# Another order for the seven block products of a matrix stage, and no low parts made by an accumulating DMA

## The chip, the cores and the metric

The kernel runs on one core of a Trainium2 chip. Times are device microseconds (us) of one execution; the profile is one further execution, taken by the hardware profiler. Five engines matter: TensorE (PE in the profile, with its weight loads as PEld), VectorE (DVE), ScalarE (ACT), GpSimd (POOL) and SyncE (SP), which here only issues DMAs. Each engine runs its instructions in program order, one behind the other, and engines wait for each other through semaphores.

## The reference

One decoder layer on 256 tokens with a width of 1024, in float32: an RMS norm and an input projection; beside each other eight attention heads (causal, with norms and rotary tables on q and k) and a gated convolution branch; an output projection added to the input; then a second RMS norm and a gated feed-forward part with 2816 inner columns. The change lies in this last part alone:

```python
x = x + jnp.concatenate([attn, conv], axis=-1) @ w_out[l]
h = rms_norm(x, norm2_g[l])
x = x + (jax.nn.silu(h @ w_gate[l]) * (h @ w_up[l])) @ w_down[l]
```

## The kernel before

**Three matmuls for one.** A float32 product is computed from two parts of each operand: a high part, rounded to the format that TensorE takes, and a low part, which is the operand less its high part. `product` (L704) issues three matmuls for it: high by high, high by low, low by high. The weights arrive in float32, 1 MB a block of 128 x 2048, and are split on the chip in *pieces* of 1024 columns, two to a block ("a" and "b"). `feed` (L248) does that. For each piece ScalarE copies the high part (`wh`, L255), and later VectorE subtracts it from the raw block for the low part (`wl`, L264). A ring holds 7 pieces. When TensorE's program reaches piece p, `feed(p + 4)` is called: it issues high parts up to p + 5 and low parts up to p + 4, the high parts first.

**How a feed-forward chunk is done.** The 2816 inner columns are cut into six chunks: 0, 1, 2, 4 and 5 of 512 columns, 3 of 256. A plain chunk (`plain_units`, L871) needs, for each of gate and up, both halves of the 1024 inputs and both halves of the 256 tokens: 8 half-block units of one piece and 4 products each. Chunks 1 and 4 are done otherwise (`shared_units`, L890), with seven block products for eight, as in Strassen's and Winograd's scheme. The activations' two token halves and two input halves are four blocks; sums of them (`xsum(0)` to `xsum(3)`) are made once by VectorE and ScalarE in `xsums_task` (L817). The weights' four blocks are gate and up by input half; in the list of pieces (`_plan`, L75) they are called b11 and b21 (gate, first and second half of the inputs) and b12 and b22 (up). Their sums are made in place: b11 becomes b11+b12, then with b22 added, then with b21 added; b12 becomes b12+b22. A sum is made either by VectorE, just before the high part of the piece (`raw`, L254), or by an accumulating DMA from HBM, issued by GpSimd just behind the low part of the piece (`raw`, L267): in the tuples of `todo` the second entry is what VectorE adds, and a pair as the third entry tells what a DMA adds, and to which block, once the piece is split.

**The order of work in a shared stage.** The loop over `STAGES` (L918) alternates: one of the seven products (2 pieces, 2 products of three matmuls each a piece), then one unit of the plain chunk beside it (1 piece, 4 products), and a last plain unit. Chunks 1 and 2 make the first shared stage, chunks 4 and 5 the second. Numbered through the kernel from 0, the first shared stage is pieces 36 to 57, the second 62 to 83; chunk 0 is 28 to 35 and chunk 3 is 58 to 61, and the last matrix follows from 84. The seven products go into three PSUM banks: U (four products), V (two) and W (one). U and V are added to on and on, and between the products a copy or a difference is taken from the bank, before the next product may write to it: `s1` and `s2` are copies of U, `s5` is a copy of V, all by ScalarE; `c11` (line L841) is W + s1, `c12` (L850) is V - s2, `c22` (L857) is s5 - U, by VectorE. `c11` goes through a silu on ScalarE and with `c12` through `times` (L795, tile `ac`); `turned` (L783) transposes such a tile on TensorE (tile `aT`, four transposes), and ScalarE and VectorE split it again (`act`, L789 and L791).

**What is put where in the queues.** Small pieces of work of this kind are generators; `step()` runs what is due after every second product, so each engine's queue is a fixed list: `feed`'s splits with this work between them. At the start of the first shared stage there still come the results of chunk 0: `up2_task` puts its two `ac` behind the splits that `feed(41)` and `feed(42)` issue, and its transposes behind piece 38 and behind piece 39 in TensorE's queue. At the second shared stage those of chunk 3 stand in the like place: `ac` behind the splits of `feed(68)`, transposes within pieces 65 and 66.

**Low parts by DMA.** In a shared stage, two of the plain chunk's low parts are not made by VectorE (the mark `"low"` in `_plan`: pieces 41 and 53, then 67 and 79). ScalarE copies the high part with its sign turned (`wl`, L261), and GpSimd issues a DMA that adds the raw block to it (L262).

**Loads.** `loads` is the order in which SP issues blocks; `load_next` is called when a piece marked "load" or "low" has been split, and issues up to the next block that lives in the ring of four `raw` buffers. b11 and b12 have buffers of their own, and so has b22 ("side", one that it shares with the tile `full`, which `xsums_task` reads). SP's queue is in order too: an issue whose buffer is still read holds up those behind it.

Of the kernel before, what the change touches and what calls it, by code (L numbers as in the profile page):

```python
# [8 lines left out]
F32 = mybir.dt.float32  # L9
# [3 lines left out]
AF = mybir.ActivationFunctionType  # L13
# [3 lines left out]
P = 128  # L17
# [4 lines left out]
W = 512  # L22
# [45 lines left out]
def _halves(c):  # L68

    if c:  # L70
        return [(z, kh, half) for z in range(2) for kh in range(2) for half in range(2)]
    return [(z, kh, half) for kh in range(2) for z in range(2) for half in range(2)]


def _plan():  # L75

    base = 14
    block = {}
    for c, width in enumerate(WIDTHS):
        for z in range(2 if width == W else 1):  # L80
            for kh in range(2):
                block[c, z, kh] = base
                base += 1
    loads = [(i, "raw") for i in range(2, 14)]
    plain = lambda i: [(i, a, None, "load") for a in range(2)]
    sources = [p for i in range(14) for p in plain(i)]
    for stage in STAGES:
        second = [(block[stage[-1], z, kh], half) for z, kh, half in _halves(stage[-1])
                  if (stage[-1], z, kh) in block]
        second_pieces = [(i, half, None, "low" if len(stage) == 2 and j % 4 == 1 else "load")  # L90
                         for j, (i, half) in enumerate(second)]
        second_loads = [(i, "raw") for i, half in second if half == 0]
        if len(stage) == 1:
            loads += second_loads
            sources += second_pieces
            continue
        b11, b21, b12, b22 = (block[stage[0], z, kh] for z in range(2) for kh in range(2))
        loads += [(b11, "big_h"), (b12, "big_l"), (b21, "raw"), second_loads[0], (b22, "side")] + second_loads[1:]
        both = [(0, 1) for _ in range(7)]
        todo = [(b11, None, None), (b21, None, "load"), (b11, b12, (b12, b22)), (b22, None, None),  # L100
                (b11, b22, (b11, b21)), (b12, None, None), (b11, None, None)]
        for j in range(8):
            if j < 7:
                i, add, then = todo[j]
                sources += [(i, a, add, then) for a in range(2)]
            sources.append(second_pieces[j])
    for i in range(base, NB):
        loads.append((i, "raw"))
        sources += plain(i)
    return loads, sources  # L110
# [66 lines left out]
def _build(nc, tc, t, ctx):  # L177
# [3 lines left out]
    raw = pool("raw", RAW)  # L181
# [5 lines left out]
    def mm_bank(name, cols=512):  # L187
        return psum.tile([P, cols], F32, name=name, tag="mm", bufs=4)

    def t_bank(name, tag="t"):  # L190
        return psum.tile([P, 512], F32, name=name, tag=tag, bufs=2)
# [15 lines left out]
    def spawn(gen, wait=0):  # L207
        tasks.append([now[0] + wait, gen])
# [10 lines left out]

    blocks, pieces = {}, []  # L220
    loads, sources = _plan()

    def load_next():
# [47 lines left out]
    def wpart(j, a):  # L271
        return [p[:, a * W:(a + 1) * W] for p in pieces[j]]
# [107 lines left out]
    c = early.tile([P, NT + 2 * NT * H], F32, name="c")  # L380
# [56 lines left out]
    def root(part):  # L437
        seed(c[:, part], v[:, part])
        newton(c[:, part], v[:, part], ca[:, part])
# [240 lines left out]
    for h in range(H):  # L680
# [6 lines left out]
        o = O[pair // 2][base:base + HD, pair % 2, :]  # L687
# [12 lines left out]
    ffn = {"r": None}  # L700
# [3 lines left out]
    def product(bank, lhs, w, start, stop, on=False):  # L704

        for a, (l, r) in enumerate(((lhs[0], w[0]), (lhs[0], w[1]), (lhs[1], w[0]))):
            nc.tensor.matmul(bank, l, r, start=start and a == 0, stop=stop and a == 2, skip_group_check=on)  # L707
        ticks[0] += 1
        if ticks[0] % 2 == 0:
            step()  # L710
# [4 lines left out]
    def residual_task(i, n):  # L715
        cols = slice(n * W, n * W + W)
        nc.vector.tensor_tensor(x2[:, i, cols], po[i, n], x2[:, i, cols], op=ALU.add)
        sq = ffn["late"].tile([P, W], F32, name=f"sq{i}{n}", tag="sum", bufs=4)
        nc.scalar.activation(sq, x2[:, i, cols], AF.Square, accum_out=sums2[:, i, n:n + 1])
        yield 0  # L720

# [30 lines left out]
    late = ffn["late"] = late_pool[0] = pool("late")  # L752
# [25 lines left out]
    def silu(name, src, i, width=W):  # L778
        s = late.tile([P, W], F32, name=name, tag="sf", bufs=3)
        nc.scalar.activation(s[:, :width], src, AF.Silu, scale=ffn["r"][:, i:i + 1])  # L780
        return s

    def turned(c, i, u, nf):  # L783
        b = t_bank(f"aT{c}{i}").rearrange("p (a q) -> p a q", a=4)
        for a in range(nf):
            nc.tensor.transpose(b[:, a, :], u[:, a * P:(a + 1) * P], ident)  # L786
        f0 = STARTS[c] // P
        hi, lo = (acts[:, z, f0:f0 + nf, tok(i)] for z in range(2))
        nc.scalar.activation(hi, b[:, 0:nf, :], AF.Copy)  # L789
        yield 1  # L790
        nc.vector.tensor_tensor(lo, b[:, 0:nf, :], hi.bitcast(F32), op=ALU.subtract)  # L791

    def times(c, i, src, s, width=W):
        u = late.tile([P, W], F32, name=f"ac{c}{i}", tag="ac", bufs=2)
        nc.vector.scalar_tensor_tensor(u[:, :width], src, ffn["r"][:, i:i + 1], s[:, :width],  # L795
                                       op0=ALU.mult, op1=ALU.mult)
        return u
# [11 lines left out]
            yield from turned(c, i, ups[i], width // P)  # L809

    def part(name):
        return late.tile([P, W], F32, name=name, tag="sum", bufs=4)

    xs = [acts[:, z, NF - 8:, :].rearrange("p f (b q) -> p (f b) q", b=2).rearrange("p (s k) q -> p s k q", s=4)
          for z in range(2)]
# [16 lines left out]
    S = {}  # L832

    def copied(name, bank):
        S[name] = part(name)
        nc.scalar.activation(S[name], bank, AF.Copy)
        yield 0

    def gate_first(c, bank):
        g = part(f"c11{c}")  # L840
        nc.vector.tensor_tensor(g, bank, S["s1"], op=ALU.add)  # L841
        yield 1
        S["g0"] = silu(f"sg0{c}", g, 0)

    def up_first(c, U, V):
        S["s2"] = part(f"s2{c}")
        nc.scalar.activation(S["s2"], U, AF.Copy)
        yield 1
        u = part(f"c12{c}")
        nc.vector.tensor_tensor(u, V, S["s2"], op=ALU.subtract)  # L850
        u = times(c, 0, u, S["g0"])
        yield 2
        yield from turned(c, 0, u, 4)

    def up_second(c, bank):
        S["u1"] = part(f"c22{c}")
        nc.vector.tensor_tensor(S["u1"], S["s5"], bank, op=ALU.subtract)  # L857
        yield 0

    def gate_second(c, bank):  # L860
        g = silu(f"sg1{c}", bank, 1)
        yield 1
        u = times(c, 1, S["u1"], g)
        yield 2
        yield from turned(c, 1, u, 4)
# [3 lines left out]
    xsum = lambda j: [[z[:, j, k, :] for z in xs] for k in range(4)]  # L869
# [20 lines left out]
    def shared_units(c):  # L890

        U, V = (t_bank(f"{n}{c}", "s") for n in "UV")
        banks = {"U": U, "V": V}

        def unit(lhs, name, start, stop, after):
            if name == "W":
                banks["W"] = mm_bank(f"W{c}")
            for k in range(4):
                if k % 2 == 0:
                    feed(at[0] + LEAD)  # L900
                product(banks[name], lhs[k], wpart(at[0], k % 2), start and k == 0, stop and k == 3, not start)
                at[0] += k % 2
            if after:
                spawn(after(), EVICT)

        todo = ((block(0, 0), "U", True, True, lambda: copied("s1", U)),
                (block(1, 0), "W", True, True, lambda: gate_first(c, banks["W"])),
                (xsum(0), "V", True, True, lambda: copied("s5", V)),
                (xsum(3), "V", False, True, None),
                (xsum(1), "U", False, True, lambda: up_first(c, U, V)),  # L910
                (xsum(2), "U", False, True, lambda: up_second(c, U)),
                (block(1, 1), "U", False, True, lambda: gate_second(c, U)))
        return [lambda u=u: unit(*u) for u in todo]

# [3 lines left out]
    for stage in STAGES:  # L918
# [9 lines left out]
        else:  # L928
            c = stage[0]
# [14 lines left out]
    for f, i, n in order:  # L944
        if i == n == 0:
            feed(at + f + LEAD)
        product(pd[i, n], [acts[:, z, f, tok(i)] for z in range(2)], wpart(at + f, n), f == 0, f == NF - 1)
        if f == NF - 1:
            o = late.tile([P, W], F32, name=f"o{i}{n}", tag="sum", bufs=4)
            nc.vector.tensor_tensor(o, pd[i, n], x2[:, i, n * W:n * W + W], op=ALU.add)  # L950
            nc.sync.dma_start(t["out"][i][:, n * W:n * W + W], o)

# [58 lines left out]
```

## Time and profile before

| | |
|---|---|
| median of 3 runs | 298.17 us (297.9 to 298.96) |
| profiled execution, its own time | 298.19 us |
| its span | 296.4 us |
| around the span | 1.79 us |
| granted TensorE clock | 1.00 |
| TensorE busy with matmuls | 287.7 us of the span |
| VectorE busy | 208.0 us |
| ScalarE busy | 176.9 us |

The views used below: the page of the profile (busy time), a table of busy time by stretch of the span, the list of waits (who waited for whom, total, number of times, longest), the chain of work that ended last, and the timeline, whose rows give start, duration, engine, line, operation, output and inputs, and in brackets how long the engine had been idle and what ended that. A "xN" at the end of a timeline row is N instructions one behind the other, merged. A row of a VectorE instruction overlaps the next by under 0.1 us, so the spacing of starts is what one costs in the queue, not its duration.

### The profile page before, as it was taken

How to read it: one execution, taken by the hardware profiler on the slowest of the kernel's cores; microseconds unless marked ns; L12 is line 12 of the kernel's file. 1: busy time of each engine (PE TensorE's matmuls, PEld its weight loads, DVE VectorE, ACT ScalarE, POOL GpSimd, SP SyncE). 2: the span in 40 equal slices, each digit the busy share in tenths (PEclk: the TensorE clock that was granted, in tenths of full speed). 3: DMA queues.
4: the chain of work that ended last, by engine and by line, in shares of the span. 5: the costliest groups of instructions: out<-in, count | busy, mean ns of one | idle time of the engine just before them, and what ended most of it. 6: DMA issues, size and time to landing. Idle time of an engine off the chain costs nothing.

```text
span 296.4 us, 3672 instructions
## 1 busy us (share of the span) xinstructions
PE 287.7 (97%) x1333; PEld 231.7 (78%) x1333; DVE 208.0 (70%) x322; ACT 176.9 (60%) x266; POOL 25.1 (8%) x46
## 2 busy tenths in 40 slices
PE   8999999999999999999998999999989999999994
PEld 6888877778788888887786788887868888888883
DVE  3899995999972967999946838989288474444111
ACT  4776768989735677768549635667676263344000
POOL 0005372000000000003111000302100000000000
PEclk9999999999999999999999999999999999999999
DMA  7999868544603449399996991599677368400012
GB/s 251 418 413 355 313 250 313 199 142 150 277 10 133 144 163 404 109 399 190 294 206 145 426 425 81 168 181 310 126 216 313 112 205 324 174 2 0 0 63 78
DMA packets 12051, 62.83 MB, mean 212 GB/s; under 512 B 1601, under 2 KB 2209, under 8 KB 6274
## 3 DMA queue, kind: packets, MB, share of 16 engines
q1 hardware_dynamic: 9874, 54.86, 48.6%
q0 software_dynamic: 2016, 7.74, 13.6%
q8 instruction: 10, 0.16, 0.2%
q14 instruction: 7, 0.06, 0.1%
q10 hardware_dynamic: 144, 0.00, 0.0%
HBM read 59.46 MB, written 1.05 MB: 204 GB/s over the span
## 4 chain that ended last, share of the span: by engine, by line
PE 79%; DMA 8%; DVE 6%; ACT 4%; issue 2%; ACTq 0%
PE pd L707 20%; PE p L668 18%; PE fg L707 17%; DMA raw<-w 8%; PE po L707 7%; PE U L707 6%; DVE wl L264 2%; ACT wh L255 2%; PE aT L786 1%; PE warm L325 1%; PE S L511 1%; PE pT L541 1%; DVE raw L254 1%; ACT act L789 1%; DVE act L791 1%
## 5 line engine op out<-in xcount | busy, mean ns | idle before, releaser
L264 DVE TENSOR_TENSOR wl<-raw,wh 128x1024 fp32r<-128x1024 f32 x98 | 117.6, 1221 | 31.4 <-ACT wh L255 31.1
L255 ACT ACTIVATE wh<-raw 128x1024 fp32r<-128x1024 f32 x102 | 105.0, 1056 | 43.7 <-PE pd L707 19.9
L707 PE MATMUL fg<-wh,g 128*128 128x512 f32 x224 | 73.1, 392 | 0.0
L707 PE MATMUL pd<-wh,act 128*128 128x512 f32 x176 | 55.2, 391 | 0.0
L707 PEld LDWEIGHTS fg<-wh,g 128*128 128x128 f32 x224 | 42.1, 188 | 8.5
L707 PE MATMUL fg<-wl,g 128*128 128x512 f32 x112 | 43.7, 390 | 0.1
L707 PEld LDWEIGHTS pd<-wh,act 128*128 128x128 f32 x176 | 33.0, 188 | 6.8
L707 PE MATMUL pd<-wl,act 128*128 128x512 f32 x88 | 34.2, 389 | 0.0
L668 PE MATMUL p<-wh,xh 128*128 128x512 f32 x80 | 33.2, 415 | 0.0
L668 PE MATMUL p<-wh,xl 128*128 128x512 f32 x80 | 31.6, 395 | 0.0
L668 PE MATMUL p<-wl,xh 128*128 128x512 f32 x80 | 26.8, 395 | 0.0
L707 PEld LDWEIGHTS fg<-wl,g 128*128 128x128 f32 x112 | 21.0, 188 | 4.7 <-DMA wl<-raw 0.6
L707 PEld LDWEIGHTS pd<-wl,act 128*128 128x128 f32 x88 | 16.5, 188 | 3.4
L789 ACT ACTIVATE act<-aT 128x512 fp32r<-128x512 f32 (+1 forms) x12 | 6.8, 564 | 19.9 <-PE aT L786 19.9
L668 PEld LDWEIGHTS p<-wh,xh 128*128 128x128 f32 x80 | 15.3, 191 | 3.7 <-issue 0.7
L791 DVE TENSOR_TENSOR act<-aT,act 128x512 fp32r<-128x512 f32 (+1 forms) x12 | 7.7, 646 | 14.7 <-ACT act L789 14.7
L668 PEld LDWEIGHTS p<-wh,xl 128*128 128x128 f32 x80 | 15.2, 191 | 3.1
L668 PEld LDWEIGHTS p<-wl,xh 128*128 128x128 f32 x80 | 15.2, 191 | 3.1 <-DVE wl L264 0.2
L262 POOL DMA_DIRECT2D wl<-raw x4 | 3.5, 887 | 135.5 <-ACT wl L261 135.5
L950 DVE TENSOR_TENSOR o<-pd,x 128x512 f32<-128x512 f32 x4 | 2.8, 692 | 14.6 <-PE pd L707 14.6
L707 PE MATMUL po<-wh,mixh 128*128 128x512 f32 x32 | 12.6, 395 | 0.0
L707 PE MATMUL po<-wh,mixl 128*128 128x512 f32 x32 | 12.5, 390 | 0.0
(172 smaller groups left out, 387.6 us busy)
## 6 DMA issues: line engine op xcount, KB each, us to landing
raw<-w SPq DMA_DIRECT2D x45, 1024.0 KB, 5.8
raw<-w POOLq DMA_DIRECT2D x8, 512.0 KB, 8.5
first<-first SPq DMA_DIRECT2D x8, 384.0 KB, 6.6
wl<-raw POOLq DMA_DIRECT2D x4, 512.0 KB, 4.7
xtok<-xtok SPq DMA_DIRECT2D x2, 512.0 KB, 9.1
x<-xtok SPq DMA_DIRECT2D x2, 512.0 KB, 7.8
out<-o SPq DMA_DIRECT2D x4, 256.0 KB, 2.0
inv<-inv POOLq DMA_DIRECT2D x1, 768.0 KB, 7.0
```

The lines of the kernel that those rows point to most:

```text
L254: nc.vector.tensor_tensor(src, src, blocks[add][:, cut(a)], op=ALU.add)
L255: nc.scalar.activation(dst[0], src, AF.Copy)
L262: nc.gpsimd.dma_start(dst[1].bitcast(F32), src, accum_op=ALU.add)
L264: nc.vector.tensor_tensor(dst[1], src, dst[0].bitcast(F32), op=ALU.subtract)
L325: nc.tensor.matmul(warm[:, 0:T], zeros[:, 0:P], zeros, start=True, stop=True)
L511: nc.tensor.matmul(banks[a][:, out], G["qT"][rows, j, q], G["kT"][rows, j, k], start=True, stop=True)
L541: nc.tensor.transpose(b[:, a * P:(a + 1) * P], p[:, a * P:(a + 1) * P], ident)
L668: nc.tensor.matmul(banks[i], (xh, xh, xl)[a][:, kt, sls[i]], w[a % 2], start=kt == 0 and a == 0, stop=kt == KT - 1 and a == 2 - (order[-1] ...
L707: nc.tensor.matmul(bank, l, r, start=start and a == 0, stop=stop and a == 2, skip_group_check=on)
L786: nc.tensor.transpose(b[:, a, :], u[:, a * P:(a + 1) * P], ident)
L789: nc.scalar.activation(hi, b[:, 0:nf, :], AF.Copy)
L791: nc.vector.tensor_tensor(lo, b[:, 0:nf, :], hi.bitcast(F32), op=ALU.subtract)
```

## The change

1. The seven products come in another order. In units of (weights, activations, bank) it was: b11 into U; b21 into W; b11+b12 into V; b22 into V; b11+b12+b22 into U; b12+b22 into U; the sum of all four into U. It becomes: b11 into U; b11+b12 into V; b11+b12+b22 into U; b21 into W; b12+b22 into U; b22 into V; the sum of all four into U. Two products of one bank now have always another bank's product between them, and two plain units. The sums that VectorE makes for pieces 42, 43, 48 and 49 (68, 69, 74 and 75 in the second stage) are now made for pieces 39, 40, 42 and 43 (65, 66, 68 and 69), and the DMA sums are issued behind those.
2. `s2` is copied by itself behind the third product (it was the first half of `up_first`); `c11` follows the fourth, `c22` the fifth and `c12` the sixth.
3. The marks "low" go: all low parts are VectorE's subtraction.
4. The loads follow the new order: the first two blocks of the plain chunk come before b22 and b21.
5. The buffers with the tag "sum" are five instead of four (2 KB more in each partition).

```diff
-        second_pieces = [(i, half, None, "low" if len(stage) == 2 and j % 4 == 1 else "load")
+        second_pieces = [(i, half, None, "load")
                          for j, (i, half) in enumerate(second)]
...
-        loads += [(b11, "big_h"), (b12, "big_l"), (b21, "raw"), second_loads[0], (b22, "side")] + second_loads[1:]
+        loads += [(b11, "big_h"), (b12, "big_l"), second_loads[0], second_loads[1], (b22, "side"),
+                  (b21, "raw")] + second_loads[2:]
         both = [(0, 1) for _ in range(7)]
-        todo = [(b11, None, None), (b21, None, "load"), (b11, b12, (b12, b22)), (b22, None, None),
-                (b11, b22, (b11, b21)), (b12, None, None), (b11, None, None)]
+        todo = [(b11, None, None), (b11, b12, (b12, b22)), (b11, b22, (b11, b21)), (b21, None, "load"),
+                (b12, None, None), (b22, None, None), (b11, None, None)]
...
-        sq = ffn["late"].tile([P, W], F32, name=f"sq{i}{n}", tag="sum", bufs=4)
+        sq = ffn["late"].tile([P, W], F32, name=f"sq{i}{n}", tag="sum", bufs=5)
...
-    def up_first(c, U, V):
-        S["s2"] = part(f"s2{c}")
-        nc.scalar.activation(S["s2"], U, AF.Copy)
-        yield 1
+    def up_first(c, V):
         u = part(f"c12{c}")
         nc.vector.tensor_tensor(u, V, S["s2"], op=ALU.subtract)
         u = times(c, 0, u, S["g0"])
...
         todo = ((block(0, 0), "U", True, True, lambda: copied("s1", U)),
+                (xsum(0), "V", True, True, lambda: copied("s5", V)),
+                (xsum(1), "U", False, True, lambda: copied("s2", U)),
                 (block(1, 0), "W", True, True, lambda: gate_first(c, banks["W"])),
-                (xsum(0), "V", True, True, lambda: copied("s5", V)),
-                (xsum(3), "V", False, True, None),
-                (xsum(1), "U", False, True, lambda: up_first(c, U, V)),
                 (xsum(2), "U", False, True, lambda: up_second(c, U)),
+                (xsum(3), "V", False, True, lambda: up_first(c, V)),
                 (block(1, 1), "U", False, True, lambda: gate_second(c, U)))
```

More of the change, by code (lines that the diff above doesn't have):

```diff
@@ L811, in part @@
     def part(name):
-        return late.tile([P, W], F32, name=name, tag="sum", bufs=4)
+        return late.tile([P, W], F32, name=name, tag="sum", bufs=5)
     xs = [acts[:, z, NF - 8:, :].rearrange("p f (b q) -> p (f b) q", b=2).rearrange("p (s k) q -> p s k q", s=4)
@@ L948, in _build @@
         if f == NF - 1:
-            o = late.tile([P, W], F32, name=f"o{i}{n}", tag="sum", bufs=4)
+            o = late.tile([P, W], F32, name=f"o{i}{n}", tag="sum", bufs=5)
             nc.vector.tensor_tensor(o, pd[i, n], x2[:, i, n * W:n * W + W], op=ALU.add)
```

## Prediction

> **What bounds the kernel now.** First the page's busy time, then busy time by stretch (the columns are PE, PEld, DVE, ACT and POOL busy us with counts, granted clock, DMA share, GB/s), then one piece of the chain that ended last.
>
> ```profile
> span 296.4 us, 3672 instructions
> PE 287.7 (97%) x1333; PEld 231.7 (78%) x1333; DVE 208.0 (70%) x322; ACT 176.9 (60%) x266; POOL 25.1 (8%) x46
> ...
> 129.00:183.00 54.00, 51.96 (x238) 41.76 (x237) 40.45 (x42) 32.36 (x38) 5.36 (x6) 1.00 0.88 273
> ...
> 187.00:231.00 44.00, 42.84 (x190) 34.43 (x190) 33.20 (x34) 29.58 (x36) 5.32 (x6) 1.00 0.83 234
> 231.00:292.00 61.00, 61.00 (x277) 50.40 (x275) 25.85 (x25) 18.32 (x19) 0.00 (x0) 1.00 0.29 103
> ...
> 169.44 6.80 PE fg L707 x30
> ```
>
> TensorE is the bound. It is idle for some us in the two shared stages (129 to 175 and 187 to 231) and not at all behind them. An undisturbed matmul costs 6.80 / 30 = 0.227 us, at a granted clock of 1.00. The change leaves the matmuls as many as they are, so all it can win is the time in which TensorE waits in the shared stages. The list of waits names them; the last line here is ScalarE's.
>
> ```profile
> PEld U L707 <- ACT s L847: 2.6, 2, 1.6
> PEld U L707 <- DVE c L857: 2.1, 2, 1.0
> ...
> PEld V L707 <- ACT s L836: 0.9, 2, 0.5
> ...
> PEld fg L707 <- DMA wl<-raw: 0.6, 1, 0.6
> ...
> ACT wh L255 <- DMA raw<-w: 6.5, 2, 3.6
> ```
>
> Three waits come twice, one in each stage: U for the copy s2, U for c22, V for the copy s5. Once a matmul waits for a low part made by DMA. The timeline around the longest shows what such a wait costs and where it comes from.
>
> ```profile
> 154.96 1.06 ACT L255 ACTIVATE wh<-raw 128x1024 fp32r<-128x1024 f32 x1 [3.56 <-DMA raw<-w]
> ...
> 155.93 1.04 ACT L261 ACTIVATE wl<-wh 128x1024 fp32r<-128x1024 f32 x1
> ...
> 158.01 0.39 PE L707 MATMUL fg<-wh,g 128*128 128x512 f32 x1
> 158.01 1.05 ACT L255 ACTIVATE wh<-raw 128x1024 fp32r<-128x1024 f32 x1
> ...
> 158.96 0.60 ACT L847 ACTIVATE s<-U 128x512 f32<-128x512 f32 x1
> ...
> 159.61 0.50 PE L707 MATMUL U<-wh,act 128*128 128x512 f32 x1 [1.21 <-ACT s L847]
> ...
> 159.94 0.40 PE L707 MATMUL U<-wl,act 128*128 128x512 f32 x1
> ```
>
> ScalarE stood still for the DMA that adds b21 to b11 (piece 54); behind that in its queue stood a low copy, another high part and then s2, and U waited for s2. From 158.01 to 159.94 two starts took 1.93 us where 2 x 0.227 = 0.45 is usual: 1.48 us lost, where the weight load's wait is listed as 1.6 (1.63 exactly). So a listed wait costs its length less 0.15 us, restart included. Seven waits: 2.6 + 2.1 + 0.9 + 0.6 - 7 x 0.15 = **5.15 us** lost in all.
>
> **What the change takes away.** In the new order one plain unit, one product into another bank and another plain unit, 12 + 12 + 12 matmuls or 36 x 0.227 = 8.2 us, lie between two products of a bank, where 12 matmuls, 2.7 us, lay before. A copy takes 0.60 us, so only a queue late by some 7 us would hold a bank. ScalarE's queue had such a hold, the 3.56 us for the DMA; its accumulate was issued after piece 48 and needed at 54. It now goes out after piece 42, still for 54, and the one for b12 goes out after 39 for 48, nine pieces ahead as before. Seven waits go: **-5.15 us**.
>
> **What it adds: VectorE.** Four low parts (41, 53, 67, 79) return to VectorE, and its sums come sooner. This matters where VectorE has no air. Its queue at the first shared stage:
>
> ```profile
> 126.27 1.22 DVE L264 TENSOR_TENSOR wl<-raw,wh 128x1024 fp32r<-128x1024 f32 x1
> 127.41 0.69 DVE L829 TENSOR_TENSOR act<-xs,act 128x512 fp32r<-128x512 f32 x1
> 128.01 2.35 DVE L264 TENSOR_TENSOR wl<-raw,wh 128x1024 fp32r<-128x1024 f32 x2
> 130.28 1.22 DVE L254 TENSOR_TENSOR raw<-raw,raw 128x1024 f32<-128x1024 f32 x1
> 131.41 0.74 DVE L795 SCALAR_TENSOR_TENSOR ac<-fg,rstd,sf 128x512 f32<-128x512 f32 x1
> 132.08 1.22 DVE L254 TENSOR_TENSOR raw<-raw,raw 128x1024 f32<-128x1024 f32 x1
> 133.21 1.22 DVE L264 TENSOR_TENSOR wl<-raw,wh 128x1024 fp32r<-128x1024 f32 x1
> 134.34 0.74 DVE L795 SCALAR_TENSOR_TENSOR ac<-fg,rstd,sf 128x512 f32<-128x512 f32 x1
> 135.01 1.22 DVE L264 TENSOR_TENSOR wl<-raw,wh 128x1024 fp32r<-128x1024 f32 x1
> ...
> 131.61 1.06 ACT L255 ACTIVATE wh<-raw 128x1024 fp32r<-128x1024 f32 x1 [2.78 <-DVE raw L254]
> ...
> 134.74 0.60 PE L786 MATMUL aT<-c_ident,ac 128*128 128x128 f32 x4
> ...
> 136.33 0.40 PE L707 MATMUL W<-wh,g 128*128 128x512 f32 x1
> 136.56 0.60 PE L786 MATMUL aT<-c_ident,ac 128*128 128x128 f32 x4
> ```
>
> Not one of these starts has an idle time before it: VectorE works without a break. The two `ac` are chunk 0's results, and TensorE transposes them at 134.74 and 136.56, right after they are made (131.41 and 134.34, 0.74 us each). In the new order `feed(38)` and `feed(39)` put the sums for 39 and 40 ahead of these, and `feed(41)` the low part of 41; the sums for 42 and 43 stand where they stood. Three instructions more come ahead of both `ac`. One costs (130.28 - 128.01) / 2 = 1.135 us in the queue. In order: sum 39 at 126.27, low 38 at 127.41, the `act` of xs at 128.54, sum 40 at 129.14, low 39 at 130.28. Low 40 must wait for its high part: sum 40 ends at 130.36, ScalarE starts 0.11 later (131.50 to 131.61 in the rows), takes 1.06, so low 40 starts near 131.53, 0.11 late. Then sum 42 at 132.67, low 41 at 133.80, the first `ac` at 134.94 (0.67 in the queue, 132.08 - 131.41), sum 43 at 135.61, low 42 at 136.74, the second `ac` at 137.88 to 138.62. The first transposes wait until 135.7 (134.74 before). The second can start near 138.65 instead of 136.56: 2.1 us late, the first wait contained in it, and 0.10 us for the restart (159.94 - 159.61 less 0.227). **+2.2 us**. Its bounds are 0, if the transposes found their tiles in time, and 8.4 (2.2 + 6.2) by the third rival below.
>
> [...]
>
> **In the second shared stage** the same three come, with air around them.
>
> ```profile
> 180.41 1.22 DVE L264 TENSOR_TENSOR wl<-raw,wh 128x1024 fp32r<-128x1024 f32 x1
> 181.92 0.69 DVE L791 TENSOR_TENSOR act<-aT,act 128x512 fp32r<-128x512 f32 x1 [0.29 <-ACT act L789]
> 183.74 0.69 DVE L791 TENSOR_TENSOR act<-aT,act 128x512 fp32r<-128x512 f32 x1 [1.14 <-ACT act L789]
> 184.35 2.35 DVE L264 TENSOR_TENSOR wl<-raw,wh 128x1024 fp32r<-128x1024 f32 x2
> ...
> 190.36 0.88 DVE L795 SCALAR_TENSOR_TENSOR ac<-fg,rstd,sf 128x256 f32<-128x256 f32 x2
> ...
> 193.84 0.38 PE L786 MATMUL aT<-c_ident,ac 128*128 128x128 f32 x2
> ```
>
> Sum 65 fills the idle 0.29 + 1.14 us ahead of 183.74. From 184.35 follow sum 66, low 65, low 66, sum 68, low 67, sum 69 and low 68: seven at 1.135, and 0.11 for a high part, bring the `ac` pair to 192.4, the first done 0.44 later. TensorE wants it at 193.84, or one matmul's 0.227 earlier for the weight load. **0**, with 0.7 us of air; without the air it costs what VectorE is later than that.
>
> **Costed at nothing.** Lows 53 and 79 and the sums that leave 48, 49, 74 and 75: in 129 to 183 VectorE is busy 40.45 of 54 us. ScalarE sheds four copies of 1.04 us. The loads: b22 is now read by sum 42, at 132.67; SP issues it at 122.41, held until `full` is read, and a load lands after 4.7 to 10.9 us, so by 133.3 at the latest, 128.2 with the median. Its cover is 10.3 us; behind that each us is one of stall, since the `ac` stand behind sum 42 (0.6 us at the slowest landing).
>
> ```profile
> 122.41 0.80 SPq L230 DMA_DIRECT2D raw<-w  x2
> ...
> DMA to landing us min/median/max: 4.7/5.8/10.9
> ...
> DMA to landing us min/median/max: 7.2/8.5/12.4
> ```
>
> The last line is for the accumulates: issued near 131.5 and 132.8, they land by 145.2. TensorE reaches piece 48 after the 24 products of pieces 39 to 47, at 3 x 0.227 each, and the new wait: 134.74 + 16.3 + 2.2 = 153.2. c12 gets a plain unit and a product, 18 matmuls, before its transposes. The fifth "sum" buffer is memory only.
>
> **The sum**, against the profiled execution's 298.19 us (0.02 above the median): 298.19 - 5.15 + 2.2 = **295.2 us**. The change gives 1.0% and keeps 2.95 of the 5.15 us that it takes away. Where VectorE's lateness is a little less or more than worked out, the result is 294.2 to 296.2.
>
> **The rivals.**
> - *No new wait.* The transposes find their tiles, all seven waits go: 298.19 - 5.15 = 293.0. For it: chunk 0's work is untouched. Against: VectorE has no idle time from 126.27 to 136.
> - *VectorE later than worked out:* one more instruction ahead of the second `ac` (1.1 us) and in the second stage the same, less its 0.7 us of air (0.4): 295.2 + 1.5 = 296.7, the edge of no change.
> - *The handoffs set the pace: slower.* With sums side by side, a low part waits for its high part, and that for its sum; VectorE idles 0.11 + 1.06 = 1.17 us each time no other instruction stands between. I count that once, covered but for 0.11. If it shows in full at 39, 40 and 42 and at 65, 66 and 68, it is 6 x 1.17 less 0.11 and less the air of 0.7: +6.2, **301.4 us**. It decides for slower once more than 2.95 + 1.5 us of it shows, five of the six. For it: ScalarE already idled for these sums (2.78 us in one row above). Against: in the program one VectorE instruction stands between each sum and its low part, and ScalarE is free.
> - *The bank waits stay,* because the copies stand in ScalarE's queue behind high parts that wait for accumulates; only the wait for the low DMA (0.45) goes: 298.19 - 0.45 + 2.2 = 299.9. Against: the accumulates have nine and twelve pieces to land.
>
> **How the numbers follow.** The forecast has 0.60, no new wait 0.13, later VectorE 0.15, handoffs 0.08, bank waits that stay 0.04. The likeliest gives 295.2. The range 293.0 to 297.0 takes in the first three, from the full gain to the later VectorE, and leaves out the two slow ones. About 0.5% (1.5 us) is what a measurement of this kernel can tell from no change, so faster means under 296.7: 0.60 + 0.13 and the near edge of the third, 0.75. The rest of the third and the weak forms of the last two are no change, 0.15; slower 0.10.
>
> **What would show it.** Right: no waits of U or V for L847, L836 or L857 in the list of TensorE's waits; new ones of `aT` (PEld) for VectorE's L795 near 135 and 137, none near 191 to 193; no "low" copies (L261) and 102 subtractions at L264; no ScalarE wait for an accumulate that TensorE feels. Wrong: TensorE waits for `wl` or `wh`, VectorE idle between the sums at 126 to 138 with ScalarE as the cause, or b22 landing past 132.7.

## The result and the profile after

The changed kernel takes 294.61 us (294.29 to 294.98), the one before in the same comparison 298.21 us (297.9 to 298.96): a ratio of 0.9876, 95% interval 0.9853 to 0.9899. The prediction was 295.2 us, between 293.0 and 297.0. The profiled execution took 294.38 us, 3.81 us less than the one of before.

The page after, then TensorE's weight-load waits (total, times, longest), then busy time by stretch (columns as before):

```profile
span 292.4 us, 3667 instructions
...
PE 285.6 (98%) x1333; PEld 231.6 (79%) x1333; DVE 213.1 (73%) x326; ACT 174.1 (60%) x262; POOL 21.4 (7%) x42
```

```profile
PEld aT L787 <- DVE ac L796: 2.6, 2, 1.3
PEld L326 <- DVE one L309: 1.0, 1, 1.0
```

```profile
129.00:183.00 54.00, 52.26 (x241) 42.73 (x240) 44.51 (x46) 33.87 (x41) 3.51 (x4) 1.00 0.76 251
187.00:231.00 44.00, 44.00 (x202) 36.34 (x201) 34.12 (x36) 29.76 (x36) 1.74 (x2) 1.00 0.63 201
```

Of the waits for L847, L857, L836 and the low DMA none is left; two for `ac` have come, both in the first shared stage, and in the second TensorE never stops. To compare the stages by themselves, without what comes ahead of them, take the first matmul into U and the last of the last matrix, from the views of the tiles U and pd ("first to last start"; line numbers after are one higher). Before, then after:

```profile
L707 PE MATMUL U<-wh,g x32: 389/389/502, 129.3 to 225.2; 128*128 128x512 f32 x32
...
L707 PE MATMUL pd<-wh,act x176: 388/389/481, 230.9 to 291.9; 128*128 128x512 f32 x176
```

```profile
L708 PE MATMUL U<-wh,g x32: 389/389/395, 128.8 to 221.1; 128*128 128x512 f32 x32
...
L708 PE MATMUL pd<-wh,act x176: 388/389/481, 227.3 to 288.3; 128*128 128x512 f32 x176
```

291.9 - 129.3 = 162.6 us has become 288.3 - 128.8 = 159.5: **3.1 us** less, of 2.95 forecast. Another 0.5 us of the profiled gain lies ahead of the first U, where TensorE's instructions are the same in both kernels; in the profiles of this study that point lies anywhere from 128.6 to 130.0. This stretch, called *the stages* from here on, is the finer measure, and it is given beside every timed result. It comes from one profiled execution of each kernel; three kernels below whose medians are the changed one's (e4, e9 and e10) read 159.5 or 159.6.

VectorE's queue after, at the place that the prediction worked out, and TensorE beside it (timeline):

```profile
125.77 1.22 DVE L255 TENSOR_TENSOR raw<-raw,raw 128x1024 f32<-128x1024 f32 x1
...
128.64 1.22 DVE L255 TENSOR_TENSOR raw<-raw,raw 128x1024 f32<-128x1024 f32 x1
129.78 2.49 DVE L265 TENSOR_TENSOR wl<-raw,wh 128x1024 fp32r<-128x1024 f32 x2
132.19 1.22 DVE L255 TENSOR_TENSOR raw<-raw,raw 128x1024 f32<-128x1024 f32 x1
133.33 1.22 DVE L265 TENSOR_TENSOR wl<-raw,wh 128x1024 fp32r<-128x1024 f32 x1
134.46 0.74 DVE L796 SCALAR_TENSOR_TENSOR ac<-fg,rstd,sf 128x512 f32<-128x512 f32 x1
...
137.39 0.74 DVE L796 SCALAR_TENSOR_TENSOR ac<-fg,rstd,sf 128x512 f32<-128x512 f32 x1
```

```profile
134.00 0.39 PE L708 MATMUL fg<-wh,g 128*128 128x512 f32 x1
135.26 0.66 PE L787 MATMUL aT<-c_ident,ac 128*128 128x128 f32 x4 [0.87 <-DVE ac L796]
...
136.93 0.40 PE L708 MATMUL V<-wh,act 128*128 128x512 f32 x1
138.19 0.66 PE L787 MATMUL aT<-c_ident,ac 128*128 128x128 f32 x4 [0.87 <-DVE ac L796]
```

With the 0.5 us by which the first U is early, the forecast starts are 125.77 for the first sum, 132.17 for sum 42, 134.44 and 137.38 for the two `ac`; the rows say 125.77, 132.19, 134.46 and 137.39. TensorE loses 1.26 - 0.23 = 1.03 us at each of the two transposes.

### The profile page after: what moved, and what is told of

It reads as the page before. It is cut to its first block, busy times and chain, and to the rows that moved or that the text cites. A ratio compares the mean times of both kernels' runs of the same rounds, so it can differ in the third digit from the quotient of the medians.

```text
span 292.4 us, 3667 instructions
## 1 busy us (share of the span) xinstructions
PE 285.6 (98%) x1333; PEld 231.6 (79%) x1333; DVE 213.1 (73%) x326; ACT 174.1 (60%) x262; POOL 21.4 (7%) x42
## 4 chain that ended last, share of the span: by engine, by line
PE 84%; DVE 10%; ACT 2%; issue 2%; DVEq 0%; ACTq 0%
PE pd L708 21%; PE p L669 18%; PE fg L708 18%; PE po L708 7%; PE U L708 7%; PE V L708 3%; DVE wl L265 3%; PE W L708 2%; DVE raw L255 2%; PE aT L787 2%; PE warm L326 1%; PE S L512 1%; PE pT L542 1%; ACT wh L256 1%; DVE g L735 1%
## 5 line engine op out<-in xcount | busy, mean ns | idle before, releaser
L265 DVE TENSOR_TENSOR wl<-raw,wh 128x1024 fp32r<-128x1024 f32 x102 | 122.7, 1221 | 24.4 <-ACT wh L256 24.0
L268 POOL DMA_DIRECT2D raw<-w x8 | 7.0, 879 | 141.4 <-DVE raw L255 86.4
```

The costliest lines, as they stand in the source:

```text
L265: nc.vector.tensor_tensor(dst[1], src, dst[0].bitcast(F32), op=ALU.subtract)
L268: nc.gpsimd.dma_start(blocks[to][:, cut(a)], t["w"][more - 2][:, cut(a)], accum_op=ALU.add)
```

## The experiments

Timed results are medians beside the kernel before on the same chip, with the ratio and its interval.

**Transposes later (e1_defer).** One line of `up2_task`:

```diff
-            yield 1
+            yield 4 if c == 0 and i else 1
```

> The changed kernel, but chunk 0's transposes stand three steps later in TensorE's queue: the first in the middle of piece 41, the second behind it (before: behind 38 and behind 39). VectorE's queue keeps its order up to the second ac. Theory (the two ac come 1.04 us late each time because VectorE works without a break, and nothing else in the front of the stage is late): both waits of aT for L796 go, 294.6 - 2.1 = 292.5 us. Rival (VectorE is late for all that TensorE needs there, and the next reader waits in their place: the low parts of 41 to 43 or the copy s1): waits of 1 to 2 us appear at wl or U, 293.6 to 294.6 us.

Measured: 292.63 us, ratio 0.9805 (0.9785 to 0.9825); the stages take 157.4 us.

```profile
L708 PE MATMUL U<-wh,g x32: 389/389/395, 129.6 to 219.8; 128*128 128x512 f32 x32
...
L708 PE MATMUL pd<-wh,act x176: 388/389/481, 225.9 to 287.0; 128*128 128x512 f32 x176
```

2.1 us less than the changed kernel's 159.5, the forecast size of the new wait. Nothing took its place: TensorE waits for nothing in either shared stage (it is busy 46.00 of the 46 us from 129 to 175, and 43.00 of the 43 from 187 to 230). The lateness was that of the two `ac` alone, and this kernel is faster than both.

**One instruction more on VectorE (e7_one_more, and e8_defer_one_more on top of e1_defer).**

```diff
+                if j == 40:
+                    nc.vector.tensor_tensor(dst[1], src, dst[0].bitcast(F32), op=ALU.subtract)
```

> The changed kernel with one instruction more on VectorE, the low part of piece 40 made twice, ahead of both ac. Theory (there is no air in that queue and TensorE waits one for one): the second aT comes 1.14 us later, 294.6 + 1.1 = 295.7 us. Rival (some of the wait has another cause): under 295.2 us.

> The kernel of e1_defer (chunk 0's transposes three steps later) with the same one instruction more as e7_one_more. Theory (with the transposes later VectorE has 1.8 us or more of air ahead of them): no wait of aT, as e1_defer, 292.6 us. Rival (VectorE is late for what follows too): 293.3 to 293.7 us.

Measured: 296.0 us (0.9935, 0.9912 to 0.9958) and 292.46 us (0.9818, 0.9797 to 0.9839); the stages 161.5 and 157.4. With the transposes where the change leaves them, one more instruction costs at least its own length; with them later, nothing (157.4 both times). The profiled execution of e7 lost more than that, 2.0 us in the stages, and its rows show why. The timeline of TensorE, then two stretches:

```profile
136.45 0.66 PE L789 MATMUL aT<-c_ident,ac 128*128 128x128 f32 x4 [2.14 <-DVE ac L798]
...
138.18 0.63 PE L710 MATMUL V<-wl,act 128*128 128x512 f32 x1
138.60 0.63 PE L710 MATMUL V<-wh,act 128*128 128x512 f32 x1
139.38 1.12 PE L789 MATMUL aT<-c_ident,ac 128*128 128x128 f32 x4
```

```profile
134.10:137.50 3.40, 1.26 (x8) 0.97 (x8) 3.40 (x5) 1.06 (x1) 0.00 (x0) 1.00 0.99 195
137.50:140.90 3.40, 3.25 (x11) 2.25 (x10) 3.40 (x5) 3.26 (x5) 1.01 (x2) 0.50 0.84 263
```

The second transposes come at 139.38, 1.2 us behind the changed kernel's 138.19, as worked out (VectorE's queue is as far behind). But the first wait, now 2.14 us in one piece, was followed by 3.4 us at a granted clock of 0.50, in which matmuls started 0.42 us apart, not 0.23. That stretch belongs to this one execution, whose mean granted clock was 0.994: the other three of e7, at 0.998 to 1.000, took 295.73 to 296.12 us, near the 295.7 expected.

**The low parts by DMA again, in the new order (e2_low_back).**

```diff
-        second_pieces = [(i, half, None, "load")
+        second_pieces = [(i, half, None, "low" if len(stage) == 2 and j % 4 == 1 else "load")
```

> The changed kernel with one part undone: the low parts of pieces 41, 53, 67 and 79 are made by the accumulating DMA again; the new order stays. Theory (the wait of the transposes is VectorE's queue, 1.135 us an instruction): low 41 leaves the queue ahead of the two ac, the second aT waits 1.1 us less in all; piece 41's low part by DMA lands near 139.1 where TensorE wants it near 139.2, so 0 to 0.4 us back: 293.5 to 293.9 us. Rival (taking the low DMAs away was worth something in the new order too, through ScalarE's copies or the DMA engines): 294.6 to 296 us.

Measured: 295.65 us (0.9904, 0.9881 to 0.9927); the stages 161.1, 1.6 us more than the changed kernel. The theory missed. Half of it held: one wait of `ac` is left, of 1.0 us (list of waits: 1.3, once), so an instruction taken off that queue gives its length back. The other half was wrong. ScalarE, GpSimd and TensorE in this kernel:

```profile
134.06 1.06 ACT L256 ACTIVATE wh<-raw 128x1024 fp32r<-128x1024 f32 x1 [1.56 <-DVE raw L255]
135.02 1.04 ACT L262 ACTIVATE wl<-wh 128x1024 fp32r<-128x1024 f32 x1
...
136.36 0.87 POOL L263 DMA_DIRECT2D wl<-raw  x1 [4.78 <-ACT wl L262]
...
139.49 0.40 PE L708 MATMUL fg<-wh,g 128*128 128x512 f32 x1
141.60 0.50 PE L708 MATMUL fg<-wl,g 128*128 128x512 f32 x1 [1.72 <-DMA wl<-raw]
```

The low copy stands behind high 42 in ScalarE's queue, and that waits for VectorE's sum 42. This was so in the kernel before, too, but now sums 39 and 40 stand ahead of sum 42, which starts 2.44 us later (132.72, before 130.28; the first U is at 129.3 in both). The DMA starts as much later, at 136.36 (before 133.92), and TensorE waits till 141.60, where the low part was expected near 139.1: 2.11 - 0.23 = 1.9 us for piece 41, and some 0.6 us for piece 67. For those of pieces 53 and 79 it doesn't wait. So the early sums and the low DMAs of pieces 41 and 67 get in each other's way.

**The low parts alone, in the old order (e3_old_order).** The same line changed the other way, in the kernel before.

> The kernel before with one part of the change alone: no low parts by DMA; order, copies and buffers as before. Theory: the wait for the low DMA goes (0.42), and in both stages the 1.04 us copy that stood between piece 54's (80's) high part and s2 leaves ScalarE's queue, so U's wait for s2 shrinks from 1.37 to 0.3 and from 0.71 to 0; c22's and s5's waits stay; low 41 adds 1.135 us ahead of the ac, within their 1.25 us of air: 298.2 - 0.4 - 1.0 - 0.8 = 296.0 us. Rival (the bank order alone carries the gain, the low parts only their own 0.42): 297.8 us.

Measured: 296.13 us (0.9923, 0.9898 to 0.9949); the stages 161.3, so 1.3 us less than before, not the 2.2 expected. The waits of this kernel:

```profile
PEld U L707 <- DVE c L857: 2.1, 2, 1.0
PEld V L707 <- ACT s L836: 1.8, 2, 1.4
...
PEld U L707 <- ACT s L847: 0.7, 1, 0.7
```

The wait for the DMA is gone and U's for s2 has shrunk from 2.6 to 0.7, near what was expected. But V's for s5 has grown from 0.9 to 1.8, in the first stage alone: low 41 makes VectorE's sum 49 later, ScalarE's high 49 waits for it, and s5 stands behind that. Counted from the first U this is 0.4 us, half of the growth; the other half is that TensorE, which no DMA holds up any more, comes there sooner. So the marks alone bring 1.3 us, and the order the other 1.8 of the 3.1, its own new wait already paid. Taken the other way round (e2), the order alone brings 1.5 us and the marks the other 1.6: what one part is worth depends on the other.

**U's last two products close together again (e4_adjacent, e5_adjacent_later).** e4 exchanges the fifth and sixth products, so that one plain unit lies between U's last two, as before. e5 does that and puts the transposes of each shared chunk's first result one step later in TensorE's queue, to where they stood in the kernel before:

```diff
-                (b12, None, None), (b22, None, None), (b11, None, None)]
+                (b22, None, None), (b12, None, None), (b11, None, None)]
...
-                (xsum(2), "U", False, True, lambda: up_second(c, U)),
                 (xsum(3), "V", False, True, lambda: up_first(c, V)),
+                (xsum(2), "U", False, True, lambda: up_second(c, U)),
...
         u = times(c, 0, u, S["g0"])
-        yield 2
+        yield 3   # e5 alone
```

> The changed kernel with the fifth and sixth products exchanged, so that U's last two products have only one plain unit between them again; all else is kept. Theory (a bank needs more than 2.7 us between two of its products because c22 stands behind a plain unit's second step): c22's wait of 0.79 + 0.11 us comes back once in each stage, 294.6 + 1.8 = 296.4 us. Rival (with VectorE and ScalarE relieved, one plain unit is enough): 294.6 us.

> The kernel of e4_adjacent (fifth and sixth product exchanged), and the transposes of the first of the two results of a shared chunk stand one step later in TensorE's queue: in the middle of the plain unit between U's last two products, where they stood in the kernel before, and not ahead of that unit. New theory (c22's wait before came from VectorE's queue, in which the act behind those transposes stands ahead of c22, and not from the bank's two products being 2.7 us apart): the wait of 0.79 + 0.11 us returns once in each stage, 294.6 + 1.8 = 296.4 us. Rival (it came from something else that the change removed): 294.6 us.

Measured: e4 294.58 us (0.9874, 0.9848 to 0.99), the stages 159.5, no wait for c22: a miss, and a useful one. e5 296.79 us (0.9963, 0.995 to 0.9975), the stages 161.4: the waits are back, some 0.9 us each. VectorE around c22 (L855) in e4, then in e5 with the weight load and the matmul that waited:

```profile
164.25 0.69 DVE L792 TENSOR_TENSOR act<-aT,act 128x512 fp32r<-128x512 f32 x1 [1.41 <-ACT act L790]
164.86 0.68 DVE L855 TENSOR_TENSOR c<-s,U 128x512 f32<-128x512 f32 x1
```

```profile
164.65 0.69 DVE L792 TENSOR_TENSOR act<-aT,act 128x512 fp32r<-128x512 f32 x1 [2.77 <-ACT act L790]
165.26 0.68 DVE L855 TENSOR_TENSOR c<-s,U 128x512 f32<-128x512 f32 x1
...
166.05 0.19 PEld L708 LDWEIGHTS U<-wh,g 128*128 128x128 f32 x1 [1.11 <-ACT wh L256]
166.08 0.47 PE L708 MATMUL U<-wh,g 128*128 128x512 f32 x1 [0.71 <-DVE c L855]
```

The profile puts the weight load's wait down to a high part on ScalarE, the matmul's to c22. It was c22: this ends at 165.94 and the load starts 0.11 us later, and in the second stage at 221.01 and 221.12, while no high part ends within 0.4 us of either load.

In both, c22 stands behind the split of a transposed tile. In e4 the transposes lie ahead of the plain unit, and TensorE's 12 matmuls cover the split and c22 (U begins at 166.19 in a trace that runs 1.0 us later than e5's). In e5 they lie in its middle, ScalarE and VectorE split them one after the other, and c22 is late. It was the place of these transposes in TensorE's queue, and so of their split ahead of c22 in VectorE's, that cost the time, not the nearness of the two products.

**Sums on GpSimd (e6_pool_sums).**

```diff
-                nc.vector.tensor_tensor(src, src, blocks[add][:, cut(a)], op=ALU.add)
+                eng = nc.gpsimd if j in (39, 40) else nc.vector
+                eng.tensor_tensor(src, src, blocks[add][:, cut(a)], op=ALU.add)
```

> The changed kernel, but the sums for pieces 39 and 40 are made by GpSimd instead of VectorE. Theory (each instruction taken off VectorE's queue ahead of the two ac gives its 1.135 us back, up to the 2.17 us lost): the two waits of aT shrink to 0 to 0.3 us if GpSimd makes a sum in under 3 us, 292.5 to 292.8 us. [...]

Measured: 297.09 us (0.9974, 0.996 to 0.9988); the stages 161.6, 2.1 us more than the changed kernel. GpSimd and VectorE:

```profile
123.39 2.77 POOL L256 TENSOR_TENSOR raw<-raw,raw 128x1024 f32<-128x1024 f32 x1 [77.51 <-DVE wl L266]
127.33 2.78 POOL L256 TENSOR_TENSOR raw<-raw,raw 128x1024 f32<-128x1024 f32 x1 [1.16 <-DVE wl L266]
...
123.83 3.42 DVE L266 TENSOR_TENSOR wl<-raw,wh 128x1024 fp32r<-128x1024 f32 x1
127.17 3.49 DVE L831 TENSOR_TENSOR act<-xs,act 128x512 fp32r<-128x512 f32 x2
```

The theory missed, though GpSimd's sum stays under the 3 us that it asked for. While GpSimd makes a sum of 2.77 us, VectorE's instruction of 1.22 us takes 3.42, and two of 0.69 take 3.49: about 2.2 us lost each time, against 1.135 taken off. VectorE's subtraction began at 123.83, 0.44 us behind GpSimd's sum, and ended 1.09 us behind it. The two `ac` come at 136.86 and 139.79 (134.46 and 137.39 in the changed kernel, whose first U is 0.4 us earlier). Why VectorE takes so long beside such a sum, the trace doesn't show.

**Two parts costed at nothing (e9_old_loads, e10_four):** the loads in their old order, and four "sum" buffers.

> The changed kernel with the loads in their old order (b21 third, b22 behind the plain chunk's first block). Theory (no load is awaited by a queue that TensorE waits for; b22 is issued at the same place, b21's buffer comes free at piece 46 for a block needed at piece 56): same as the changed kernel, 294.6 us, and 159.5 to 159.7 us from the first matmul into U to the last matmul. Rival (the order of loads is needed by the new order): a wait of wh for raw reaches TensorE, 295.5 us or more.

> The changed kernel with four buffers of the tag sum again. Theory (with s1, s5, s2 and c11 in them, c22 takes s1's place after c11 and c12 takes s5's after c22, both free before they are wanted): same, 294.6 us, and 159.5 to 159.7 us from the first matmul into U to the last matmul. Rival (a fifth is needed, since s2 and c11 wait for a buffer that VectorE still reads): 295 us or more.

Measured: 294.66 us (0.9868, 0.9839 to 0.9897) and 294.59 us (0.9865, 0.9837 to 0.9894); the stages 159.5 and 159.6. Neither part carries any of the time.

## Why the prediction was right, and where its reasons were not

- *The seven waits, -5.15 us:* right in sum. None is left after, and e1, in which TensorE waits for nothing in the two stages, has them 162.6 - 157.4 = 5.2 us shorter than the kernel before. The reason given, that 36 matmuls lie between two products of a bank where 12 lay before, was too simple. For c22, e4 shows that 12 are enough; what it waited for was the split of transposes ahead of it in VectorE's queue (e5). The new order happens to put c22 far ahead of that split: in the first stage it starts at 156.58, and those transposes come at 167.26. The prediction didn't name this, so for c22's part of the sum it was right by luck. For s2 the hold in ScalarE's queue was named and is confirmed by e3, where U's wait shrinks to 0.7 once a copy and part of the DMA's lateness (3.56 us before, 1.80 in e3) are gone. For s5, e3 shows that its wait goes by what stands ahead of it in ScalarE's queue; no run shows how far the 36 matmuls were needed.
- *VectorE's three instructions ahead of the `ac`, +2.2 us:* right, 2.07 us by the rows, the queue within 0.02 us at the starts that were compared, and the sum that reads b22 (132.19) found its block there. An instruction costs 1.135 us in that queue after as before ((134.46 - 132.19) / 2). e1 takes the lateness away and gains 2.1; e7 adds one and e2 takes one off, and the `ac` follow one for one. VectorE makes 102 subtractions, as forecast, 98 before.
- *The second shared stage, 0 with 0.7 us of air:* right. After, the pair stands in VectorE's queue at 190.91, its first is done near 191.35, and TensorE transposes at 192.31:

```profile
188.64 1.22 DVE L255 TENSOR_TENSOR raw<-raw,raw 128x1024 f32<-128x1024 f32 x1
189.77 1.22 DVE L265 TENSOR_TENSOR wl<-raw,wh 128x1024 fp32r<-128x1024 f32 x1
190.91 0.87 DVE L796 SCALAR_TENSOR_TENSOR ac<-fg,rstd,sf 128x256 f32<-128x256 f32 x2
...
192.31 0.38 PE L787 MATMUL aT<-c_ident,ac 128*128 128x128 f32 x2
```

- *Handoffs that set the pace:* one shows, low 40's, as counted (the two rows merged at 129.78 take 2.41 us to the next start, not 2.27). *Bank waits that stay* and *no new wait* fell with the rows above; e1 is the kernel in which the latter holds, and it takes 292.6, where 293.0 was given.
- *The 0.6 us between 295.2 and 294.61:* some 0.1 in the stages (2.07 in place of 2.2), and about 0.5 ahead of the first U in the profiled execution, a point that moves by up to 1.4 us between profiles. That this explains the medians isn't shown; the kernel before alone has medians of 297.88 to 298.63 us in the comparisons of this study.

## What to carry to other kernels

Where an engine's queue runs without a break, an instruction put in ahead of a result that another engine wants costs its full spacing once the air is used up (here three instructions of 1.135 us cost 2.07 us, since before, the second result was done 1.48 us ahead of its transposes; in e8, where there is air, one more costs nothing). This can be worked out from the starts in one trace; the cheap mend is often to ask for the result later, here three steps further down TensorE's queue, for 2.1 us. Before a wait is put down to two users of one buffer being close together, look at what stands ahead of the awaited instruction in its own queue: moving that may be enough. Work moved to an idle engine need not be free: with the two sums on GpSimd (e6), VectorE lost about 2.2 us beside each, where 1.135 us was taken off its queue.

## What was not expected of the hardware

- A wait of TensorE of 2.14 us in one piece (e7) was followed by 3.4 us at half the granted clock, and some 0.8 us were lost beyond the wait (2.0 less 1.2). In e6 the wait was longer, and no such stretch followed in the profiled execution. The timeline of TensorE in e6, then one stretch:

```profile
137.65 0.66 PE L788 MATMUL aT<-c_ident,ac 128*128 128x128 f32 x4 [2.86 <-DVE ac L797]
```

```profile
134.10:137.50 3.40, 0.70 (x4) 0.23 (x2) 3.40 (x4) 1.06 (x1) 0.00 (x0) 1.00 1.04 204
```

So neither the length of the wait alone nor the busy time of some 3.4 us decides it: TensorE was busy 1.26 us in the stretch of e7 after which the clock fell, and only 0.70 in this one of e6, after which it didn't. It also differs between executions of one kernel. Of the ten timed executions of e6, six had a mean granted clock of 0.993 or 0.994, as e7's profiled one had, and took 297.08 to 298.14 us; the other four, at 0.997 to 1.000, took 296.2 to 296.96. No trace shows where the clock fell in those six, and no run shows what makes it fall.
- GpSimd's sum of 128 x 1024 took 2.77 us, against VectorE's 1.22, and VectorE's instructions beside it took about 2.2 us longer than elsewhere (3.42 us in place of 1.22 beside the first).
